# Two parts of a norm in one tile, and four operand tiles that begin 8, 16 or 24 bytes later

## The chip, the core and the metric

One core of a Trainium2 chip runs the kernel. The metric is the device time of one execution in microseconds; for the kernel before it is the median of three runs. A second source is one profiled execution, whose trace gives every instruction's start and duration, engine by engine. Engines are named as the profile names them: PE is TensorE's matmul row, PEld the row of its weight loads, DVE is VectorE, ACT ScalarE, POOL GpSimd, SP the engine whose queue issues most loads.

## The reference

256 tokens of width 1024 pass through two blocks. What matters here is where a norm's output is used as a matmul operand:

```
n1   = rmsnorm(h, norm1_g);  proj = n1 @ w_in          # first block, 40 weight tiles
n2   = rmsnorm(h, norm2_g);  peer: n2 @ w_q, then n2 . expert_u for 128 x 128 experts
x    = x + 0.5 * g1x * swiglu(modulate(rmsnorm(x)), w13_ffn1, w2_ffn1)     # same for ctx
u    = modulate(rmsnorm(x)) @ w_in_2                   # "XN"; the same for ctx, "XC"
x    = x + 0.5 * g3x * swiglu(modulate(rmsnorm(x)), w13_ffn2, w2_ffn2)
out  = rmsnorm(x, norm_final)
```

## The kernel before

Everything lies feature-major: 128 features on the partitions, 8 feature chunks, 256 tokens along the free dimension. Each fp32 operand is split into a high and a low fp32r part (hi + lo), and a product takes three matmuls: hi by whi, lo by whi, hi by wlo (lines 249 to 251). The weights stream through three `raw` buffers of 128 x 1024; ACT copies each to `whi` (line 112), DVE takes the remainder as `wlo` (line 113). A weight tile then serves 24 matmuls of 256 token columns, one weight load of 128 columns each. The order of the work is a list written out by hand; `Emit.run` walks through it, so nothing is scheduled anew.

Five kinds of tiles supply the moving columns or the stationary weights that this case is about. A norm's output is the pair `nhi`, `nlo` made by `npair`: n1 in the first block, n2 for the queries and the 128 expert tiles, then a pair for the context's first norm, then XN for the second block's mixing stage, all in the same place one after the other. `y` is the unnormed product x times gain with two more columns for the modulation's shift, 258 in all: both feed-forward stages start on it before their norm is known (`ypair`, `unit_y`); the context's mixing norm XC lies in the same tile with 256 columns. `nxh`, `nxl` hold the feed-forward's normed input, `ah`, `al` (and `mh`, `mch`, `fohi`, `mhi` and the like) the inputs of the products behind. In the `tm` products (lines 425 to 427) the norm is the stationary operand and 512 columns of weights move.

Tiles are allocated at multiples of 32 bytes of a partition, and the table `GAP` puts unused tiles of 64 to 192 bytes ahead of some. Worked out from the program: `whi` and `wlo` begin 96 bytes past a multiple of 256, n, y, ah, al, mch, fo and m 32 bytes past a multiple of 256, all of them so 32 bytes past a multiple of 64, and a chunk of a norm (1024 bytes) or of y (1280 bytes) keeps that.

Of the kernel before, what the change touches and what calls it, by code (L numbers as in the profile page):

```python
# [12 lines left out]
F32R = mybir.dt.float32r  # L13
# [7 lines left out]
P = 128  # L21
T = 256
D = 1024
KD = D // P
# [12 lines left out]
TS = 320  # L37

GAP = {"n": 48, "ya": 40, "y": 48, "mc": 0, "nx": 32, "q": 48, "v": 16, "sc": 48, "y01": 0, "fo": 40, "f2": 32, "mh": 48}

NE = 7

# [160 lines left out]
def body(ctx, tc, I, out):  # L203
# [6 lines left out]
    npool = ctx.enter_context(tc.tile_pool(name="npool", bufs=1))  # L210
# [17 lines left out]
    def table(func):  # L228

        act.activation(out=dummy, in_=one, func=func)  # L230
# [5 lines left out]
    def V(name):  # L236
        w = dict(VEC)[name]
        return vec[:, VOFF[name]:VOFF[name] + w]
# [16 lines left out]
    def scr(wk, shape=(P, 512)):  # L255
        return wk.tile(list(shape), F32, name="scr", tag="scr", bufs=NSCR[wk.name])


    def ones_sum(qs, bank=bankB):
        ps = bank()  # L260
        for j, q in enumerate(qs):
            for a in range(2):
                pe.matmul(ps[:, :T], ones, q[:, a * T:a * T + T], start=j + a == 0, stop=a == 1 and j == len(qs) - 1)  # L263
        return ps
# [60 lines left out]
    def late_norm(x, r, gain, n, of, when, shift=None, lag=1):  # L325

        def f(d):
            hi, lo = n()
            t = of(d)
            dve.scalar_tensor_tensor(out=t, in0=x[:, d, :], scalar=gain[:, d:d + 1], in1=r, op0=ALU.mult, op1=ALU.mult)  # L330
            if shift is None:
                em.later(lambda: act.copy(hi[:, d, :], t))
                em.later(lambda: dve.tensor_tensor(out=lo[:, d, :], in0=t, in1=hi[:, d, :], op=ALU.subtract), lag)
                return
            sh = shift[:, d:d + 1]
            em.later(lambda: act.activation(out=hi[:, d, :], in_=t, func=AF.Identity, bias=sh))
            em.later(lambda: dve.scalar_tensor_tensor(out=lo[:, d, :], in0=t, scalar=sh, in1=hi[:, d, :],
                                                      op0=ALU.add, op1=ALU.subtract), lag)
        for d in range(KD):
            if when is None:  # L340
                f(d)
            else:
                em.later(lambda d=d: f(d), when[d])
# [7 lines left out]
    def root(ps, scale=1.0 / D, bias=None):  # L351
        r = npool.tile([P, T], F32, name="rr", tag="rr", bufs=1)
        act.activation(out=r, in_=ps[:, :T], func=AF.Sqrt, bias=(eps if bias is None else bias)[:, 0:1], scale=scale)
        return r
# [14 lines left out]
    def gap(pl, name):  # L369
        if GAP[name]:  # L370
            pl.tile([P, GAP[name]], F32, name="gap" + name, tag="gap" + name)

    def chunked(t, w, first=0):

        step = T if w == T else TS
        return t[:, first:first + KD * step].rearrange("p (k t) -> p k t", k=KD)[:, :, 0:w]

    def npair(pl, tag):
        return [chunked(pl.tile([P, KD * T], F32R, name=tag + n, tag=tag + n), T) for n in ("hi", "lo")]

    def apair():
        return [npool.tile([P, T], F32R, name=n, tag=n, bufs=2) for n in ("ah", "al")]
# [206 lines left out]
    hT = {}  # L589
# [62 lines left out]
            nc.sync.dma_start(out=kT[n], in_=I[("k1", "k2")[n]])  # L652

    gap(npool, "n")
    n1 = npair(npool, "n")

    def begin(fetch):
        his, lows, squares, S["q"] = parts(x0, V("norm1_g"), Y1(), pa)
# [334 lines left out]
    def norm2():  # L993
        S["r"] = root(ones_sum(S["q"][:1]))
        table(AF.Gelu_apprx_tanh)
        dve.reciprocal(out=S["r"], in_=S["r"])
        hT["n2"] = npair(npool, "n")
        late_norm(hres, S["r"], V("norm2_g"), X2, lambda d: hres[:, d, :], [0, 0, 0, 0, 0, 1, 1, 1])

    units += [("w", I["wo"][k], wout(k)) for k in range(KD)]  # L1000
# [292 lines left out]
    def first_units(sp):  # L1293
        ps = [q_bank(n) for n in range(2)]
        mm3s([p[:, :T] for p in ps], sp, *Y1(), T)
        em.later(norm2, 1)
# [10 lines left out]
    for j in range(NQ, 16):  # L1307
        n = min(j - 1, sc + (3 if j > NQ else 0))
# [50 lines left out]
    def flat(t):  # L1359
        return t.rearrange("p a t -> p (a t)")  # L1360
# [46 lines left out]
    E_ = {}  # L1407
    Ex = ExitStack()

    def open_pd():  # L1410
        Gx.close()
        Sx.close()
        pd = Ex.enter_context(tc.tile_pool(name="pd", bufs=1))
        E_["p"] = pd
        E_["x"] = pd.tile([P, KD, T], F32, name="x")
        h1 = pd.tile([P, KD, T], F32, name="h1")
        E_["h1"] = h1
        pool.dma_start(out=h1, in_=hD)


        fg = V("final_g")
        w = pd.tile([P, KD], F32, name="w", tag="gain", bufs=3)
        dve.tensor_tensor(out=w, in0=fg, in1=fg, op=ALU.mult)
        dve.tensor_scalar(out=w, in0=w, scalar1=EPS, scalar2=None, op0=ALU.add)
        E_["w"] = E_["x"][:, 0:4, :].rearrange("p a (b i) -> p (a b) i", i=P)
        dve.tensor_copy(E_["w"], w.unsqueeze(2).to_broadcast([P, KD, P]))
        g = gain_of(pd, "norm_ffn1_2", 8)
        dve.tensor_tensor(out=g, in0=g, in1=fg, op=ALU.mult)
        E_["g"] = g
        open_d()  # L1430
        E_["y"] = ypair()
        shift_parts(0, E_["y"])

    def ypair(width=T + 2):
        y = M["p"].tile([P, 2 * KD * TS], F32R, name="y", tag="y", bufs=1)
        return chunked(y, width), chunked(y, width, KD * TS)

    def done_c():
        pd, x, h1, fg = E_["p"], E_["x"], E_["h1"], V("final_g")
# [55 lines left out]
    def nc_pair():  # L1495
        B["n"] = npair(npool, "n")

    second = [ev(b) for b in range(64, P - 2)]
    n = len(ADA_A)
# [22 lines left out]
    def add_to_x(acc, hg):  # L1522
        x = E_["x"]

        def add(d):
            dve.scalar_tensor_tensor(out=x[:, d, :], in0=acc.o(d), scalar=hg[:, d:d + 1], in1=x[:, d, :],
                                     op0=ALU.mult, op1=ALU.add)
        return add
# [28 lines left out]
    M = {}  # L1557
# [32 lines left out]
    def x_sums(func):  # L1590

        em.later(lambda: qsum(E_["q"]))

        def f():
            E_["r"] = root(ones_sum(E_["q"][:1], bankA))
            table(func)
            dve.reciprocal(out=E_["r"], in_=E_["r"])
        em.later(f, 3)

    def f1_done(acc):  # L1600
        x = E_["x"]
        add = add_to_x(acc, E_["hg"])
        for d in ORDER:
            add(d)

        def squares():
            table(AF.Sqrt)
            E_["q"] = [scr(E_["p"]) for _ in range(4)]
            for j, q in enumerate(E_["q"]):
                act.activation(out=q, in_=flat(x[:, 2 * j:2 * j + 2, :]), func=AF.Square)  # L1610
            x_sums(AF.Exp)

        def norm():
            E_["n"] = npair(npool, "n")
            late_norm(x, E_["r"], E_["g"], XN, lambda d: scr(E_["p"])[:, :T], range(KD), modx[:, 24:32])
        em.later(squares, 1)
        em.later(norm, 9)
# [16 lines left out]
    def ctx_done():  # L1634
        hg = E_["p"].tile([P, KD], F32, name="hgc")
        dve.tensor_scalar(out=hg, in0=modc[:, 16:24], scalar1=0.5, scalar2=None, op0=ALU.mult)
        for d in ORDER:
            dve.scalar_tensor_tensor(out=M["ctx"][:, d, :], in0=accc.o(d), scalar=hg[:, d:d + 1],
                                     in1=M["ctx"][:, d, :], op0=ALU.mult, op1=ALU.add)
        M["nc"] = ypair(T)  # L1640
        a, q, b, c = ctx_norm("norm_mix_2", 24, lambda: M["ctx"], lambda: [scr(E_["p"]) for _ in range(4)], XC)
        em.later(lambda: (table(AF.Sqrt), a()))
        em.later(q, 1)
        em.later(lambda: (b(AF.Exp), c(range(KD))), 4)
# [304 lines left out]
    def mixout(k):  # L1949
        def fn(hi, lo):  # L1950
            if k == KD - 3:
                x_prep("norm_ffn2_2", 48, 40, 1.0, lambda: ypair())
            accm.step(hi, lo, M["m"][0][:, k, :], M["m"][1][:, k, :], k == 0, k == KD - 1)
            if k == KD - 1:
                x_parts(accm)
        return fn
# [153 lines left out]
def _program(arrays):  # L2110
    nc = _bacc.Bacc("TRN2", target_bir_lowering=False, num_devices=1)
    aps = {n: nc.dram_tensor(n + "_dram", v.shape, F32, kind="ExternalInput").ap() for n, v in arrays.items()}
    out = nc.dram_tensor("out_dram", (P, KD, T), F32, kind="ExternalOutput").ap()
    with _tile.TileContext(nc) as tc:
        body(tc, aps, out)
    return nc
# [8 lines left out]
```

## Time and profile before

| | |
|---|---|
| median of 3 runs | 1956.73 us (1954.03 to 1963.48) |
| the profiled execution's own time | 1958.64 us |
| its span | 1956.9 us |
| PE busy | 1943.4 us of the span, 15,348 matmuls |
| DVE, ACT, POOL busy | 1392.2, 1016.6, 153.2 us |
[...]

Matmuls overlap: one of 256 columns is shown with 276 to 288 ns, but the next begins some 0.11 us after it starts. What counts is the pace, from start to start. In a window, the count of instructions holds those that begin in it and the two or so that are still running when it opens.

### The profile page before, as it was taken

The page shows a single profiled execution, that of the slowest core. Times are in us where ns is not written, and L with a number is a line of the kernel's source. Part 1 is how long each engine was busy: PE and PEld are TensorE (multiplying, and loading weights), DVE is VectorE, ACT ScalarE, POOL GpSimd, SP SyncE. Part 2 cuts the span into 40 slices and gives each one's busy share as a digit, 9 for nine tenths or more (in the row PEclk, how much of TensorE's full clock was granted, in tenths as well). Part 3 has the DMA queues.
Part 4 walks back from the last instruction along what each step waited for, and adds up shares of the span by engine and source line. Part 5 has one row for each costly group of instructions (what it writes and reads, how often), then busy time and mean ns, then how long its engine had stood idle before and what let it go on. Part 6 is the DMA issues. An engine that isn't in the chain of part 4 may idle for free.

```text
span 1956.9 us, 37794 instructions
## 1 busy us (share of the span) xinstructions
PE 1943.4 (99%) x15348; PEld 1865.1 (95%) x15348; DVE 1392.2 (71%) x2282; ACT 1016.6 (52%) x1510; POOL 153.2 (8%) x296
## 2 busy tenths in 40 slices
PE   9999999999999999999999999999999999999998
PEld 8899999999999999999998888899999999999998
DVE  7667788987776776798866776489754556578555
ACT  6554645467776555545573323246654445455444
POOL 0000011111112001111000000010000000000000
PEclk9999999999999999999999999999999999999999
DMA  7656577776667778897755666677643334456653
GB/s 244 198 166 187 183 230 230 248 223 197 200 199 248 246 242 275 281 298 248 220 186 192 186 199 211 201 249 272 191 130 92 115 110 130 153 174 185 189 188 119
DMA packets 110094, 393.18 MB, mean 201 GB/s; under 512 B 14103, under 2 KB 14487, under 8 KB 109536
## 3 DMA queue, kind: packets, MB, share of 16 engines
q1 hardware_dynamic: 85968, 310.55, 50.6%
q0 software_dynamic: 22944, 77.52, 12.1%
q8 instruction: 120, 1.97, 0.4%
q10 hardware_dynamic: 1008, 2.70, 0.4%
q14 instruction: 54, 0.44, 0.1%
HBM read 371.84 MB, written 18.87 MB: 200 GB/s over the span
## 4 chain that ended last, share of the span: by engine, by line
PE 95%; DVE 2%; ACT 1%; DMA 1%; issue 0%; SPq 0%; DVEq 0%; ACTq 0%
PE wk L249 18%; PE wk L251 18%; PE wk L250 18%; PE acc L250 10%; PE acc L251 10%; PE acc L249 10%; PE acc L425 2%; PE acc L427 2%; PE acc L426 2%; PE acc L1255 1%; PE acc L1256 1%; DVE wlo L113 1%; ACT whi L112 1%; DMA raw<-w_dram 0%; PE wk L263 0%
## 5 line engine op out<-in xcount | busy, mean ns | idle before, releaser
L113 DVE TENSOR_TENSOR wlo<-raw,whi 128x1024 fp32r<-128x1024 f32 x587 | 716.6, 1224 | 463.5 <-ACT whi L112 462.3
L112 ACT CAST whi<-raw 128x1024 fp32r<-128x1024 f32 x587 | 615.6, 1050 | 652.5 <-PE wk L250 285.6
L249 PE MATMUL wk<-nhi,whi 128*128 128x256 f32 x1648 | 464.2, 282 | 0.0
L250 PE MATMUL wk<-nlo,whi 128*128 128x256 f32 x1648 | 456.4, 277 | 0.0
L251 PE MATMUL wk<-nhi,wlo 128*128 128x256 f32 x1648 | 456.2, 277 | 0.0
L250 PE MATMUL acc<-al,whi 128*128 128x256 f32 x1376 | 383.2, 279 | 0.2 <-DVE al L386 0.2
L249 PE MATMUL acc<-ah,whi 128*128 128x256 f32 x1376 | 383.1, 278 | 0.0
L251 PE MATMUL acc<-ah,wlo 128*128 128x256 f32 x1376 | 382.9, 278 | 0.0
L249 PEld LDWEIGHTS wk<-nhi,whi 128*128 128x128 f32 x1648 | 309.7, 188 | 0.9 <-issue 0.5
L250 PEld LDWEIGHTS wk<-nlo,whi 128*128 128x128 f32 x1648 | 310.0, 188 | 0.5 <-issue 0.5
L251 PEld LDWEIGHTS wk<-nhi,wlo 128*128 128x128 f32 x1648 | 309.8, 188 | 0.0
L250 PEld LDWEIGHTS acc<-al,whi 128*128 128x128 f32 x1376 | 260.2, 189 | 1.7 <-DVE al L386 0.8
L249 PEld LDWEIGHTS acc<-ah,whi 128*128 128x128 f32 x1376 | 258.3, 188 | 0.9
L251 PEld LDWEIGHTS acc<-ah,wlo 128*128 128x128 f32 x1376 | 259.0, 188 | 0.0
L249 PE MATMUL wk<-nxh,whi 128*128 128x512 f32 (+1 forms) x544 | 189.2, 348 | 0.0
L251 PE MATMUL wk<-nxh,wlo 128*128 128x512 f32 (+1 forms) x544 | 188.4, 346 | 0.0
L250 PE MATMUL wk<-nxl,whi 128*128 128x512 f32 (+1 forms) x544 | 187.4, 344 | 0.0
L385 ACT CAST ah<-early 128x256 fp32r<-128x256 f32 x128 | 52.1, 407 | 157.1 <-PE acc L251 155.3
L251 PEld LDWEIGHTS wk<-nxh,wlo 128*128 128x128 f32 x544 | 102.1, 188 | 14.1
L250 PEld LDWEIGHTS wk<-nxl,whi 128*128 128x128 f32 x544 | 103.1, 190 | 12.6
L249 PEld LDWEIGHTS wk<-nxh,whi 128*128 128x128 f32 x544 | 102.2, 188 | 11.5
L1269 POOL DMA_DIRECT2D uD<-act x128 | 69.1, 540 | 366.9 <-ACT act L1268 306.6
(526 smaller groups left out, 3343.5 us busy)
## 6 DMA issues: line engine op xcount, KB each, us to landing
raw<-pu_dram SPq DMA_DIRECT2D x128, 512.0 KB, 3.9
raw<-pv_dram SPq DMA_DIRECT2D x128, 512.0 KB, 4.4
row<-ada_dram POOLq DMA_DIRECT2D x59, 512.0 KB, 4.6
raw<-f13a_dram SPq DMA_DIRECT2D x44, 512.0 KB, 3.5
raw<-f2a_dram SPq DMA_DIRECT2D x44, 512.0 KB, 4.6
raw<-f13b_dram SPq DMA_DIRECT2D x44, 512.0 KB, 3.6
raw<-w_dram SPq DMA_DIRECT2D x41, 512.0 KB, 4.1
uD<-act POOLq DMA_DIRECT2D x128, 128.0 KB, 3.9
```

What stands on the lines that cost most here:

```text
L112: nc.scalar.copy(hi, r)
L113: nc.vector.tensor_tensor(out=lo, in0=r, in1=hi, op=ALU.subtract)
L249: pe.matmul(o, whi, xhi, start=start, stop=False)
L250: pe.matmul(o, whi, xlo, start=False, stop=False)
L251: pe.matmul(o, wlo, xhi, start=False, stop=stop)
L385: act.copy(hi, src)
L425: pe.matmul(o, xh[:, k, ts], hi[:, sl], start=k == 0, stop=False)
L426: pe.matmul(o, xh[:, k, ts], lo[:, sl], start=False, stop=False)
L427: pe.matmul(o, xl[:, k, ts], hi[:, sl], start=False, stop=k == KD - 1)
L1255: pe.matmul(o, p2[:, k, :, t], ph[:, k, :, t], start=True, stop=False)
L1256: pe.matmul(o, p2[:, k, :, t], p1[:, k, :, t], start=False, stop=True)
L1269: pool.dma_start(out=uD[:, b, :], in_=u)
```

## The change

`npair` made two tiles, one for each part; it now makes one tile of both parts and 64 elements more, and both parts begin `off` elements further on in it. `ypair` does the same with its tile, which held both parts already. `OFF` gives the elements of 4 bytes: n1 begins 8 bytes later, n2 16, XN 24, y and XC 16. The context's first norm and the pairs `fo` and `m` get the one tile and no offset.

```
+OFF = 2, 4, 6, 4
...
-    def npair(pl, tag):
-        return [chunked(pl.tile([P, KD * T], F32R, name=tag + n, tag=tag + n), T) for n in ("hi", "lo")]
+    def npair(pl, tag, off=0):
+        t = pl.tile([P, 2 * KD * T + 64], F32R, name=tag, tag=tag)
+        return [chunked(t, T, off + n * KD * T) for n in range(2)]
...
-    n1 = npair(npool, "n")
+    n1 = npair(npool, "n", OFF[0])
...
-        hT["n2"] = npair(npool, "n")
+        hT["n2"] = npair(npool, "n", OFF[1])
...
-        y = M["p"].tile([P, 2 * KD * TS], F32R, name="y", tag="y", bufs=1)
-        return chunked(y, width), chunked(y, width, KD * TS)
+        y = M["p"].tile([P, 2 * KD * TS + 64], F32R, name="y", tag="y", bufs=1)
+        return chunked(y, width, OFF[3]), chunked(y, width, OFF[3] + KD * TS)
...
-            E_["n"] = npair(npool, "n")
+            E_["n"] = npair(npool, "n", OFF[2])
```

No instruction is added, removed or moved. Put side by side engine by engine, with the tiles' new names and the line numbers taken as equal, the two programs have the same 22,626 instructions in the same order, and every wait is on the same semaphore for the same value. What differs is where tiles lie. The spare 256 bytes push everything that is allocated later along: ah, al and the first block's tiles by 256 bytes, the tiles above y by 512, the last ones by 1024. Those stay 32 bytes past a multiple of 256 where they were; n1, n2, XN, XC and y do not.

## Rows read from the trace of the kernel before

**Rows 1.** The page's first lines: span, busy time and instructions of each engine.

```profile
span 1956.9 us, 37794 instructions
PE 1943.4 (99%) x15348; PEld 1865.1 (95%) x15348; DVE 1392.2 (71%) x2282; ACT 1016.6 (52%) x1510; POOL 153.2 (8%) x296
```

**Rows 2.** The page's chain that ended last, by engine.

```profile
PE 95%; DVE 2%; ACT 1%; DMA 1%; issue 0%; SPq 0%; DVEq 0%; ACTq 0%
```

**Rows 3.** Windows, PE alone: stretch, its length, busy (count), granted clock, DMA, GB/s.

```profile
260.00:300.00 40.00, 40.00 (x355) 1.00 0.79 248
640.00:700.00 60.00, 60.00 (x532) 1.00 0.77 245
...
850.00:890.00 40.00, 40.00 (x342) 1.00 0.89 290
1766.00:1776.00 10.00, 10.00 (x85) 1.00 0.69 215
1830.00:1930.00 100.00, 100.00 (x852) 1.00 0.60 188
```

**Rows 4.** Groups by line and shape, 77 to 150 us: count, busy us, mean ns.

```profile
L251 PE MATMUL wk<-nhi,wlo 128*128 128x256 f32 x160 | 44.7, 280 | 0.0
```

**Rows 5.** The same view, 219 to 630 us.

```profile
L249 PE MATMUL wk<-nhi,whi 128*128 128x256 f32 x1071 | 302.3, 282 | 0.0
L250 PE MATMUL wk<-nlo,whi 128*128 128x256 f32 x1071 | 296.2, 277 | 0.0
L251 PE MATMUL wk<-nhi,wlo 128*128 128x256 f32 x1071 | 296.0, 276 | 0.0
```

**Rows 6.** The same view, 1353 to 1650 us.

```profile
L251 PE MATMUL wk<-nhi,wlo 128*128 128x256 f32 x336 | 92.9, 277 | 0.0
L250 PE MATMUL wk<-nlo,whi 128*128 128x256 f32 x336 | 92.9, 276 | 0.0
```

**Rows 7.** The same view of the whole run: products on y, and a plain fp32 one.

```profile
L249 PE MATMUL wk<-y,whi 128*128 128x258 f32 x104 | 29.7, 286 | 0.0
...
L318 PE MATMUL wk<-y,whi 128*128 128x258 f32 x32 | 7.9, 287 | 0.5 <-ACT y L289 0.5
...
L251 PE MATMUL acc<-y,wlo 128*128 128x258 f32 x24 | 6.8, 284 | 0.0
...
L263 PE MATMUL wk<-scr,ones 128*128 128x256 f32 x28 | 6.8, 381 | 0.1
```

**Rows 8.** The same view, 1810 to 1945 us.

```profile
L249 PE MATMUL wk<-nxh,whi 128*128 128x256 f32 x224 | 62.9, 281 | 0.0
...
L251 PE MATMUL acc<-ah,wlo 128*128 128x256 f32 x142 | 39.9, 281 | 0.0
```

**Rows 9.** The same view, 629 to 785 us.

```profile
L249 PE MATMUL acc<-ah,whi 128*128 128x256 f32 x455 | 125.6, 276 | 0.0
```

**Rows 10.** The same view, 785 to 900 us.

```profile
L250 PE MATMUL acc<-al,whi 128*128 128x256 f32 x327 | 91.9, 281 | 0.2 <-DVE al L386 0.2
```

**Rows 11.** Instructions of PE in order of time, about 788 us: start us, duration us.

```profile
788.10 0.28 PE L249 MATMUL acc<-ah,whi 128*128 128x256 f32 x1
788.36 0.38 PE L250 MATMUL acc<-al,whi 128*128 128x256 f32 x1
788.58 0.28 PE L251 MATMUL acc<-ah,wlo 128*128 128x256 f32 x1
788.70 0.28 PE L249 MATMUL acc<-ah,whi 128*128 128x256 f32 x1
788.82 0.28 PE L250 MATMUL acc<-al,whi 128*128 128x256 f32 x1
```

**Rows 12.** Instructions on tile cslh: count, duration ns min/median/max, first and last start.

```profile
L249 PE MATMUL wk<-cslh,fth x16: 280/286/290, 1686.4 to 1702.8; 128*128 128x258 f32 x16
```

**Rows 13.** In order of time, about 1764.8 us: three plain fp32 matmuls of a sum.

```profile
1764.78 0.81 PE L263 MATMUL acc<-scr,ones 128*128 128x256 f32 x3
```

**Rows 14.** Instructions on tile nlo: those of DVE that write it.

```profile
L333 DVE TENSOR_TENSOR nlo<-x,nhi x8: 417/418/420, 213.5 to 217.0; 128x256 fp32r<-128x256 f32 x8
```

## The prediction

> **What bounds the kernel now.** I read the page first: PE is busy for 1943.4 of 1956.9 us [rows 1], and the chain that ended last lies on PE for 95% of the span [rows 2]. So the kernel's time is the number of matmuls times their pace, and stalls are small change. Since the change leaves every instruction, order and wait as it was, it can only act by the pace, that is by how fast PE takes its operands from the new places.
>
> The next question is whether the pace is a constant. It is not. A window's count, less the two matmuls that run when it opens, gives it [rows 3]: 40 us by 353 is 113.3 ns from start to start while n2 moves (260 to 300), 60 by 530 is 113.2 ns with ah (640 to 700), but 40 by 340 is 117.6 ns with the very same ah, al and weight buffers at 850 to 890, and 100 by 850 is 117.6 ns in the last feed-forward. [...] There are a fast pace and a slow one, 4.3 ns apart. By groups the same shows as a mean of 276 ns [rows 9] against 281 ns [rows 10], so a group's mean tells which pace a stage had: 276 is fast, 281 is slow, what lies between is a mixture.
>
> What picks the pace is seen at 788 us [rows 11]. Ahead of it starts are 0.11 us apart. Then two matmuls are 0.26 and 0.22 us late, and from there on starts are 0.12 us apart; the mean over the stage behind it is 281 [rows 10]. Same tiles, same bytes: the pace is a state that a pause sets and that then holds. I read it as two streams, the moving columns and the next matmul's weights, that either fall in step or get in each other's way. That is a reading, and no row proves it. With 258 columns the pace is slower again: 10 us by 83 is 120.5 ns on y [rows 3], 7.2 more than the fast pace for two more columns, where 258/256 alone would ask for 0.9.
>
> **The change, part by part.** Nothing is removed or added; each moved stream is priced by what it can gain or lose in pace.
>
> The tile y, 16 bytes on. Its 258-column matmuls are 312 at lines 249 to 251 into wk (three rows like the first), 96 at lines 318 to 323 and 72 into acc, 480 in all [rows 7], means 284 to 287. At the fast pace they would take 113.3 x 258/256 = 114.2 ns instead of 120.5: 6.3 ns by 480, 3.0 us. No row shows 258 columns at the fast pace, so the lower bound of the gain is nothing; the loss, if the new place were as bad again as two more columns, is 7.2 by 480, 3.5 us.
>
> n1, 8 bytes on: 480 matmuls with mean 280 against 276 [rows 4, 9], a gain of 4 ns by 480, 1.9 us if all turn fast; a loss of 2.9 ns each (120.5 less 117.6) would be 1.4 us.
>
> n2, 16 bytes on: 3,213 matmuls between 219 and 630 us, means 277 and 276, so nearly all fast already [rows 5]. (The 282 of line 249 I put down to late starts behind the small fp16 products that stand between, which stay.) The gain left is at most 1 ns each, 3.2 us; I take 1.0. The loss, if they all turned slow, is 4.3 by 3,213, 13.8 us. This is the largest single price in the change.
>
> XN, 24 bytes on: 1,008 moving matmuls with means 277 and 276 [rows 6]: 0.5 us to gain, 4.3 us to lose.
>
> The streams behind. A pace that is set holds until the next pause, and behind y in the last feed-forward come 672 matmuls on nx (three rows of 224) and 528 on ah (22 weight tiles of 24), slow at 281 [rows 8]. If y's stream falls in step, some of these follow: 4.3 by 1,200 is 5.2 us for all of them. The rows give examples of both states after a pause, so I take half, 2.6 us. On the same ground the expert stage may go either way: its 1,365 matmuls ahead of 785 us are fast, the 980 behind it mostly slow [rows 9, 10]. That is 5.9 us to lose and 4.2 to gain, and I take nothing.
>
> The writers. ACT and DVE write the parts to the moved places, 418 ns for a low part [rows 14], and lie beside matmuls; with PE busy 99% they have time to spare [rows 1]. Eight such pieces for each of two parts and four norms: even 5% on each would be 64 x 21 ns, 1.3 us, and under the cover nothing. The tiles that move by 256, 512 or 1024 bytes keep their place within 256; I take nothing for them, by the fact that ah's two buffers (1024 bytes apart) share one mean [rows 9].
>
> The sum: 3.0 + 1.9 + 1.0 + 0.5 + 2.6 = 9.0 us. The profiled execution's 1958.64 us would become 1949.6; it lies 1.9 above the median of the runs, and from that median, 1956.73, the same 9.0 us give 1948.
>
> [...] One piece of the trace reads a 258-column operand from 8 bytes past a multiple of 64: the second half of cslh, whose first half (1032 bytes) begins at such a multiple. Both halves together last 280 to 290 ns with median 286 [rows 12], no other than y's 284 to 287 from its 32 bytes [rows 7]. So 8 bytes cost nothing there that two more columns had not cost already. [...]
>
> **The rivals.**
> *No effect.* Pace depends on where a pause falls, not on bytes, and the states come out as before: 1957, between 1952 and 1962. For it speaks that ah has both paces from one place [rows 9, 10]; against it, that instructions, and so nearly all pauses, are the same in both kernels, so that only places could change anything. [...]
>
> [...]
>
> *Slower.* n2 falls out of step. At 4.3 ns each its 3,213 matmuls cost 13.8 us, with XN's 4.3 it is 18.1: 1975. For it: the whole of n2's stage, with all its pauses for the fp16 products, is fast now from 32 bytes, so that this place looks safe and any other may be less so. From 2,100 slow matmuls on (9.0 by 4.3) it outweighs the forecast's gain. If 16 bytes cost n2 as much as the two columns cost y, it is 7.2 by 3,213, 23 us, and 1980 or more.
>
> **How the numbers follow.** The forecast (slow streams among the moved ones turn fast, fast ones stay): 0.41, 1948, own range 1940 to 1955. Below the fast pace: 0.20, 1925 to 1943. No effect: 0.18. Slower: 0.21, 1965 to 1982. Runs of this kernel spread by some 0.5%, about what tells a change from none, so the classes' bounds are 1947 and 1966.5. About half of the forecast's chance lies under 1947 (0.20) and all of the floor rival's: faster 0.40. The rest of the forecast and no effect make same 0.39, and 0.21 is slower. The range is 1932 to 1974: below it lies a third of the floor rival (0.07), above it the worse half of the slower one (0.11).
>
> **What would show it.** Right: PE's instructions and waits as before, y's means near 278 instead of 284 to 287, n1's near 276, n2's and XN's unchanged, nx's and ah's in the last feed-forward partly 276. [...] The slower one: n2's lines at 281 or more. No effect: all means within 1 ns. The forecast is wrong above all if the pace follows the place in a way the rows cannot show, since every large operand now lies 32 bytes past a multiple of 64.

## The result, and the profile after

The changed kernel took 1980.35 us (median of four runs, 1978.14 to 1981.53), the kernel before 1958.22 beside it (four runs, 1954.03 to 1963.48): a ratio of 1.0114, with an interval of 1.0093 to 1.0135. It is slower by about 22 us. The profiled execution took 1979.81 us, 21.2 more than that of before.

The page of the changed kernel, where it answers to [rows 1, 2]: span, busy time of the engines, and the chain that ended last.

```profile
span 1978.1 us, 37794 instructions
PE 1962.4 (99%) x15348; PEld 1881.7 (95%) x15348; DVE 1392.8 (70%) x2282; ACT 1017.2 (51%) x1510; POOL 153.8 (8%) x296
...
PE 96%; DVE 2%; DMA 1%; ACT 1%; issue 0%; DVEq 0%; ACTq 0%
```

The same instructions and the same chain on PE, with DVE and ACT within 0.6 us of before: what is longer is PE's busy time, by 19.0 of the 21.2 us. So the pace has changed, and the windows tell where. PE alone, as in [rows 3]:

```profile
260.00:300.00 40.00, 40.00 (x338) 1.00 0.76 234
650.00:710.00 60.00, 60.00 (x532) 1.00 0.79 241
1792.00:1802.00 10.00, 10.00 (x84) 1.00 0.66 211
1860.00:1950.00 90.00, 90.00 (x797) 1.00 0.63 194
```

The granted clock is 1.00 in all four, as in [rows 3], and 0.999 in the mean of both profiled executions, so it is not the clock. With n2 moving, 40 us by 336 is 119.0 ns from start to start, where it was 113.3. With ah, whose place stayed, 60 by 530 is 113.2 ns as before. On the 258 columns of y, 10 by 82 is 122 ns (120.5 before). The last feed-forward, 90 by 795, is 113.2 ns where it was 117.6. Groups by line and shape of n2's stage (222 to 646 us), as in [rows 5]:

```profile
L251 PE MATMUL wk<-n,whi 128*128 128x256 f32 x1066 | 306.8, 288 | 0.0
L252 PE MATMUL wk<-n,whi 128*128 128x256 f32 x1066 | 301.2, 283 | 0.0
L253 PE MATMUL wk<-n,wlo 128*128 128x256 f32 x1065 | 300.7, 282 | 0.0
```

All three means are 6 ns higher than before. This is no mixture of the old fast and slow paces: no mean lies under 282, where the slow pace had 281 [rows 8, 10], and the 119.0 ns from start to start lie above the slow pace's 117.6. XN (1369 to 1675 us), 276 and 277 before [rows 6], likewise:

```profile
L252 PE MATMUL wk<-n,whi 128*128 128x256 f32 x334 | 94.6, 283 | 0.0
...
L253 PE MATMUL wk<-n,wlo 128*128 128x256 f32 x333 | 94.1, 283 | 0.0
```

n1 (77 to 148 us), 280 before [rows 4], and its matmuls in order of time (start us, duration us). One group's mean is up by 1 ns only, but the starts tell: from the first row to the last are nine steps in 1.08 us, 120 ns each.

```profile
L252 PE MATMUL wk<-n,whi 128*128 128x256 f32 x160 | 45.6, 285 | 0.0
L253 PE MATMUL wk<-n,wlo 128*128 128x256 f32 x159 | 44.7, 281 | 0.0
```

```profile
139.77 0.28 PE L251 MATMUL wk<-n,whi 128*128 128x256 f32 x1
139.89 0.28 PE L252 MATMUL wk<-n,whi 128*128 128x256 f32 x1
...
140.85 0.28 PE L251 MATMUL wk<-n,whi 128*128 128x256 f32 x1
```

The last feed-forward (1835 to 1965 us), 281 before [rows 8], and y's 258 columns in the whole run [rows 7]:

```profile
L251 PE MATMUL wk<-nxh,whi 128*128 128x256 f32 x224 | 61.8, 276 | 0.0
...
L253 PE MATMUL acc<-ah,wlo 128*128 128x256 f32 x141 | 38.9, 276 | 0.0
```

```profile
L251 PE MATMUL wk<-y,whi 128*128 128x258 f32 x104 | 29.8, 286 | 0.0
```

A finer account comes from the starts in the two traces. For each stage the mean step from one matmul's start to the next was taken (steps over 135 ns, that is pauses, left out; for 512 columns over 270), and the difference multiplied by the stage's count:

| stage | matmuls | ns before | ns after | us |
|---|---|---|---|---|
| n1 (8 bytes) | 480 | 116.6 | 120.1 | +1.7 |
| n2 (16) | 3,216 | 113.9 | 119.2 | +17.1 |
| XN (24) | 1,152 | 113.7 | 120.7 | +8.1 |
| XC (16) | 192 | 113.7 | 119.0 | +1.0 |
| norms as stationary operand, 512 columns | 624 | 229.7 | 232.0 | +1.4 |
| y, 258 columns (16) | 480 | 120.8 | 121.6 | +0.4 |
| ah in the expert stage (not moved) | 3,072 | 114.5 | 113.4 | -3.5 |
| nx and ah of the last feed-forward (not moved) | 1,200 | 117.8 | 113.4 | -5.3 |

The moved streams lose 29.7 us, the two streams at their old places gain 8.8, and the smaller streams together another 1.1. So the paces account for 19.8 of the profiled 21.2 us; the other 1.4 is left to pauses.

### The profile page after: what moved, and what is told of

Same layout as the page of the kernel before. It is cut to its first block, busy times and chain, and to the rows that moved or that the text cites. A ratio compares the mean times of both kernels' runs of the same rounds, so it can differ in the third digit from the quotient of the medians.

```text
span 1978.1 us, 37794 instructions
## 1 busy us (share of the span) xinstructions
PE 1962.4 (99%) x15348; PEld 1881.7 (95%) x15348; DVE 1392.8 (70%) x2282; ACT 1017.2 (51%) x1510; POOL 153.8 (8%) x296
## 4 chain that ended last, share of the span: by engine, by line
PE 96%; DVE 2%; DMA 1%; ACT 1%; issue 0%; DVEq 0%; ACTq 0%
PE wk L251 19%; PE wk L253 18%; PE wk L252 18%; PE acc L252 10%; PE acc L253 10%; PE acc L251 10%; PE acc L428 2%; PE acc L429 2%; PE acc L430 2%; PE acc L1258 1%; PE acc L1259 1%; DMA raw<-pv_dram 1%; DVE wlo L115 1%; ACT whi L114 0%; PE wk L265 0%
## 5 line engine op out<-in xcount | busy, mean ns | idle before, releaser
L251 PE MATMUL wk<-n,whi 128*128 128x256 f32 x1648 | 472.7, 287 | 0.0
L252 PE MATMUL wk<-n,whi 128*128 128x256 f32 x1648 | 466.0, 283 | 0.0
L253 PE MATMUL wk<-n,wlo 128*128 128x256 f32 x1648 | 464.9, 282 | 0.0
L252 PEld LDWEIGHTS wk<-n,whi 128*128 128x128 f32 x1648 | 312.4, 190 | 0.5 <-issue 0.5
L251 PEld LDWEIGHTS wk<-n,whi 128*128 128x128 f32 x1648 | 311.1, 189 | 0.9 <-issue 0.5
L253 PEld LDWEIGHTS wk<-n,wlo 128*128 128x128 f32 x1648 | 311.6, 189 | 0.0
```

The lines of the kernel that those rows point to most:

```text
L251: pe.matmul(o, whi, xhi, start=start, stop=False)
L252: pe.matmul(o, whi, xlo, start=False, stop=False)
L253: pe.matmul(o, wlo, xhi, start=False, stop=stop)
```

## The experiments

Two theories stood first. *Boundary*: an operand must begin at a multiple of 32 bytes. *Relation*: PE's pace depends on how far the moving operand lies from the stationary weights that are loaded meanwhile (PEld is busy for 95% of the span beside PE's 99% [rows 1]); before, that distance was 192 bytes modulo 256 for all streams of 256 and 258 columns (32 less 96, worked out from the program). Where 512 columns move, it was 64. The rival to both was that the shared tile or the 256 bytes of push cost the time. Worked out from the programs, all kernels below have the instructions of before in the same order with the same waits, and differ in addresses alone; so a time that differs is not due to how their tiles are cut. In all of them the line numbers are a few off those of before, and where no other is given the kernel is the changed one with the edit shown. A pace is read from a window as above, length by count less two; where a whole stage's pace is given, it is the mean step as in the table above.

**e1, no offsets.** What is left of the change is the shared tile and the push.

```
-OFF = 2, 4, 6, 4
+OFF = 0, 0, 0, 0
```

> One tile for both parts, as in the change, but all four offsets 0; everything behind still pushed by 256 bytes or more. Boundary theory (a moving operand that does not begin at a multiple of 32 bytes is read slower, whatever the weights' place): 1957 us, n2's three lines at 276 to 282 ns as before. Relation theory (the pace follows the distance between moving operand and weights): the same, since the distance is that of before. Rival, the push: the shared tile or the 256 bytes cost the time, then about 1980 here too. Rival, chance: the states of pace fall anew, 1950 to 1965.

Measured: 1955.79 us (1952.99 to 1964.89), ratio to before 0.9993 (0.9977 to 1.0010). n2's groups (222 to 646 us) and a window of it:

```profile
L253 PE MATMUL wk<-n,wlo 128*128 128x256 f32 x1071 | 296.3, 277 | 0.0
```

```profile
260.00:300.00 40.00, 40.00 (x355) 1.00 0.78 249
```

n2 is back at 113.3 ns. The shared tile and the push cost nothing; the offsets are the whole loss. In this execution nx and ah of the last feed-forward went at 113.3 and 113.5 ns too, with both operands at the places (modulo 256) where before had 117.8: their gain in the changed kernel is no effect of the offset. Seven of the kernels here (the changed one, e1, e2, e4, e7, e8 and e9) have nx and ah at the very same addresses, and this stage took 113.4 ns in five of them and 117.8 and 117.6 in e2 and e7; so one place has both paces. That the pace also changes from one execution of one kernel to the next is not shown, since each kernel has one trace, but the spread of their times goes with it. Against e1's profiled execution, 1952.99 us, in which those streams were fast too, the changed kernel's is 26.8 us longer: the moved streams cost more than the 21.2, and the states gave some of it back.

**e2, every offset 32 bytes**, so that all moved operands begin at a multiple of 32, even of 64.

```
-OFF = 2, 4, 6, 4
+OFF = 8, 8, 8, 8
```

> All four offsets 8 elements, 32 bytes: the moved tiles begin at a multiple of 64 instead of 32 past it. Boundary theory with 32 bytes: 1957 us, 1950 to 1963, n2 at the fast pace of 113 ns. [...] Relation theory: the distance to the weights is off by 32, more than in the change, so 1975 or more and n2 over 281 ns.

Measured: 1979.10 us (1978.29 to 1981.27), ratio 1.0098 (1.0081 to 1.0115). The window in n2:

```profile
260.00:300.00 40.00, 40.00 (x340) 1.00 0.75 239
```

40 by 338 is 118.3 ns. A round address doesn't help, so the boundary theory fell.

**e3, the weights 32 bytes on and the moving operands where they were.** A pad of 32 bytes ahead of the weight buffers, and the pad ahead of the norms shortened by as much.

```
-GAP = {"n": 48, ...
+GAP = {"w": 8, "n": 40, ...
-OFF = 2, 4, 6, 4
+OFF = 0, 0, 0, 0
...
+    splp.tile([P, GAP["w"]], F32, name="gapw", tag="gapw", bufs=1)
```

> Offsets 0; the weight tiles whi and wlo lie 32 bytes further on (128 past a multiple of 256 instead of 96) and the unused tile ahead of n is 32 bytes smaller, so that nothing else moves. Boundary theory: 1957 us, 1950 to 1963, all groups as before. Relation theory: all streams change their distance to the weights, so the means of n, ah, nx and y all move, by 20 us or more in the time.

Measured: 1999.06 us (1997.13 to 2001.12), ratio 1.0198 (1.0180 to 1.0215). Windows in n2 and in ah's stage:

```profile
260.00:300.00 40.00, 40.00 (x343) 1.00 0.76 238
660.00:720.00 60.00, 60.00 (x508) 1.00 0.73 232
```

117.3 ns with n2 and, pauses included, 118.6 with ah. No moving operand was touched, and every stream of 256 columns that had gone at the fast pace became slower, ah as well, which no offset of the change reaches; the last feed-forward, slow before, stayed about where it was, 117.5 ns against 117.8. It is the weights' place relative to the moving operand, or else the weights' own place; e5 tells these apart.

**e4, the doses mixed:** n1 4 bytes, n2 8, XN 16, y 24.

```
-OFF = 2, 4, 6, 4
+OFF = 1, 2, 4, 6
```

> Offsets 1, 2, 4, 6 elements: n1 4 bytes, n2 8, XN 16, y and XC 24. In the change the paces read 120.0 ns at 8 bytes (n1), 119.2 at 16 (n2), 120.7 at 24 (XN). Boundary theory: the pace goes with the offset, not with the stage: n2 now 120.0, XN 119.2, n1 about 120; time 1980 to 1988. Stage or chance theory: n2 keeps 119.2 and XN 120.7 whatever the offset.

Measured: 1988.02 us, one run (before had a median of 1959.88 beside it). The window in n2:

```profile
260.00:300.00 40.00, 40.00 (x335) 1.00 0.74 234
```

n2 at 8 bytes goes at 120.1 ns, what n1 had from there; XN at 16 bytes at 119.1 (mean of its steps), what n2 had from there; n1 at 4 bytes at 121.6. The price belongs to the offset and not to the stage.

**e5, weights and moving operands 32 bytes on together.**

```
-OFF = 2, 4, 6, 4
+OFF = 0, 0, 0, 0
...
+    splp.tile([P, 8], F32, name="gapw", tag="gapw", bufs=1)
```

> Offsets 0; the weights and every moving tile lie 32 bytes further on together, so that all begin at a multiple of 64 and every distance is that of before. Relation theory (the pace follows the distance of moving operand and weights modulo 64): 1957 us, 1950 to 1965, n2 at 113.3 ns a matmul. Rival, absolute places (each operand wants to begin 32 bytes past a multiple of 64): about 2000 us as with the weights moved alone, n2 at 118.

Measured: 1959.85 us (1954.15 to 1964.43), ratio 1.0015 (1.0000 to 1.0031). The window in n2:

```profile
260.00:300.00 40.00, 40.00 (x355) 1.00 0.79 249
```

113.3 ns. The weights lie where e3 had them and the moving operands where e2 had n2, and each of those alone cost 1 to 2%. Together they cost nothing that can be told: of the place what counts, for steps of 32 bytes, is the distance.

**e6, weights and norms 16 bytes on, by larger weight tiles.**

```
-OFF = 2, 4, 6, 4
+OFF = 4, 4, 4, 4
-                hi = self.split.tile([P, 1024], F32R, name="whi", tag="whi")
+                hi = self.split.tile([P, 1040], F32R, name="whi", tag="whi")[:, 4:1028]
```

(`wlo` likewise, and the pad ahead of the norms shortened to 16 elements.)

> All four offsets 16 bytes, and the weights begin 16 bytes further on too (each weight buffer is 64 bytes larger, the unused tile ahead of n smaller, the rest stays modulo 256). Relation theory: n1, n2, XN and XC are back at 113.3 (or the slow state's 117.8) ns, while ah, nx, mch, fo, m, which stay, go to about 119 ns; time near 1990. Absolute theory: n2 stays at 119, and the weights off a multiple of 32 slow the rest too, 2000 or more.

Measured: 2001.20 us, one run (before had a median of 1955.97 beside it). The window in n2:

```profile
260.00:300.00 40.00, 40.00 (x341) 1.00 0.75 232
```

118.0 ns, and ah 282 in the mean: a miss. I had taken the distance modulo 64. The six buffers, now 64 bytes longer each, began 48, 112, 176 or 240 bytes past a multiple of 256, so that the norms had the old distance modulo 64 but mostly not modulo 256. That form of the theory fell; e7 and e10 try the other. The trace shows a limit of the other form: in a third of n2's weight tiles two matmuls out of three lay at the distance 192, and from the first of them to the second it took 117.5 ns in the mean (353 steps). So two matmuls at a good distance, between others that are not, don't bring the fast pace back.

**e7, multiples of 64 bytes:** n1 64, n2 128, XN 192, y 64.

```
-OFF = 2, 4, 6, 4
+OFF = 16, 32, 48, 16
```

> Offsets 64, 128, 192 and 64 bytes (n1, n2, XN, y and XC): all distances keep their value modulo 64 and change modulo 256. Relation modulo 64: 1957 us, 1950 to 1965, n2 113.3 to 113.9 ns, XN 113.7. Relation modulo 256: n1 and y (now at the weights' own place modulo 256) or n2 and XN leave 113.3, by 4 ns or more, 2 to 14 us.

Measured: 1978.29 us (1977.50 to 1980.07), ratio 1.0113 (1.0093 to 1.0134). The window in n2:

```profile
260.00:300.00 40.00, 40.00 (x342) 1.00 0.77 237
```

117.6 ns at 128 bytes; n1 at 64 had 119.9, XN at 192 had 119.0. A period of 64 bytes or of 128 would have made at least one of them fast throughout, as XN and n2 are in e1; one of 256 is not excluded, since e1's push moved tiles by 256, 512 and 1024 at no cost.

**e8, n2's offset alone.**

```
-OFF = 2, 4, 6, 4
+OFF = 0, 4, 0, 0
```

> Only n2 keeps its 16 bytes; n1, XN, y at 0. Relation theory: n2 at 119.2 ns against 113.9, 3216 matmuls, so 16.8 us slower than before, 1970 to 1977, and XN, n1 as before. Chance: n2 near 114 or other stages changed.

Measured: 1976.83 us (1969.70 to 1977.00), ratio 1.0108 (1.0087 to 1.0128). The window in n2:

```profile
260.00:300.00 40.00, 40.00 (x338) 1.00 0.75 237
```

XN's group (1369 to 1675 us), 277 before as well:

```profile
L253 PE MATMUL wk<-n,wlo 128*128 128x256 f32 x336 | 92.9, 277 | 0.0
```

n2 goes at 119.0 ns as with the whole change, while n1 (116.6) and XN (113.7) had their paces of before. n2 alone carries 17.1 us. The profiled execution, the fastest of the four, is accounted for: 1958.64 + 17.1, less 5.3 for a last feed-forward at 113.4 ns, is 1970.4, and it took 1969.70.

**e9, four more distances:** n1 96 bytes, n2 248, XN 160, y 240.

```
-OFF = 2, 4, 6, 4
+OFF = 24, 62, 40, 60
```

> Offsets 96, 248, 160 and 240 bytes: the distance from the weights to the moving operand, modulo 256, is 32 for n1, 184 for n2, 96 for XN and 176 for y and XC (192 in the kernel before). Distance theory modulo 256 with 192 as the one good place: all four slower than before, n2 119 to 122 ns a matmul, XN and n1 117 to 120, y's 256-column products 119 or so, time 1975 to 1990. Rival: 192 is only one good place of several, then one of these stages shows 113.3 ns.

Measured: 1980.18 us, one run beside 1961.34 of before. The window in n2:

```profile
260.00:300.00 40.00, 40.00 (x335) 1.00 0.74 232
```

120.1 ns at n2's distance of 184, 8 short of the good one (it also begins 8 past a multiple of 16, of which e12 tells more); XN at 96 bytes of distance had 120.0, XC at 176 had 119.3, n1 at 32 had 117.2. There was no second good place among them.

**e10, the weights follow the norms by 16 bytes**, with all six weight buffers cut from one tile, so that they stay 1024 bytes apart. n1, n2, XN and y are 16 bytes on too; ah, nx, fo and m stay behind.

```
-OFF = 2, 4, 6, 4
+OFF = 4, 4, 4, 4
...
+        t = self.split.tile([P, 6 * 1024 + 8], F32R, name="w", tag="w", bufs=1)
+        self.w = [t[:, 4 + 1024 * i:4 + 1024 * (i + 1)] for i in range(6)]
...
-                hi = self.split.tile([P, 1024], F32R, name="whi", tag="whi")
+                hi = self.w[ns % 3 + 0]
```

(`wlo` likewise, and the pad ahead of the norms shortened by 32 bytes.)

> All four offsets 16 bytes, and all six weight buffers 16 bytes further on as well (cut from one tile, so that all stay alike modulo 256); ah, nx, mch, fo, m stay. Distance theory modulo 256: n1, n2, XN and XC are back at distance 192 and at the paces of before, n2 113.9 ns; ah, nx, mch, fo and m come to distance 176 and leave 113.3 (113.4 for ah in the expert stage) for 118 to 121. Rival, the moved tiles' own places are what is slow: n2 stays at 119.2 and ah at 113.4 to 114.5.

Measured: 1978.40 us, one run beside 1961.34. Windows in n2 and in ah's stage, and n2's group (230 to 600 us):

```profile
260.00:300.00 40.00, 40.00 (x355) 1.00 0.80 247
660.00:720.00 60.00, 60.00 (x508) 1.00 0.76 232
```

```profile
L255 PE MATMUL wk<-n,w 128*128 128x256 f32 x976 | 268.6, 275 | 0.0
```

The loss has changed sides: n2 goes at 113.3 ns from the very place that cost it 17 us, and ah, which nobody moved, at 118.6. With before and the changed kernel this makes all four pairs of weights at 96 or 112 past a multiple of 256 and moving operand at 32 or 48: fast at 96 with 32 and 112 with 48, slow at the other two. It is the cleanest evidence for the distance, in one run and its trace. It shows another thing: n1 had 113.9 here, under the 116.6 it had before.

**e11, everything 16 bytes on**, weights, norms, y, ah, nx, mc, mh and the small tiles, each cut from a tile with `SH` elements ahead; every distance is again that of before. Its core, beyond e10:

```
+    SH = 4
...
+        if "t" not in AP:
+            AP["t"] = npool.tile([P, 4 * T + 64], F32R, name="a", tag="a")
+        n = AP["n"] = 1 - AP.get("n", 1)
+        return [AP["t"][:, SH + T * k:SH + T * k + T] for k in (n, 2 + n)]
```

> Everything moves together: the weights and every moving tile (n, y, ah, al, nx, mc, fo, m, mh, the branches' y, y01, y23) begin 16 bytes further on, so that each distance to the weights is that of the kernel before. Distance theory alone: 1957 us, 1950 to 1965, fast and slow states mixed as before, 0.998 to 1.002. If at this place the fast state also holds better, as the 114 to 113.4 ns of n1, XN and the 227 ns of the 512-column products in the run with weights and norms moved by 16 hint: 1935 to 1950, with ah and nx at 113.3 in most stages. Absolute places: over 1975.

Measured: 1940.30 us (six runs, 1939.10 to 1942.45), ratio to before 0.9916 (0.9901 to 0.9931): faster than both kernels. Windows, and nx's group of the last feed-forward (1800 to 1940 us):

```profile
260.00:300.00 40.00, 40.00 (x356) 1.00 0.81 256
660.00:720.00 60.00, 60.00 (x532) 1.00 0.78 242
```

```profile
L255 PE MATMUL wk<-nx,w 128*128 128x256 f32 x224 | 61.6, 275 | 0.0
```

n2 and ah were fast before and are so here. The gain is that nearly nothing is slow any more: n1 116.6 to 114.0 ns, nx with 512 columns 229.2 to 227.0, ah of the first feed-forward 117.7 to 114.6, all from the mean steps, and the last feed-forward 113.4 against the 117.8 that before had in its profile.

**e12, the same with 8 bytes**, to tell distance from place.

```
-SH = 4
+SH = 2
```

> The same with 8 bytes instead of 16. Distance theory alone: 1957 us, 1950 to 1965. [...]

Measured: 2032.87 us (2032.24 to 2034.22), ratio 1.0390 (1.0369 to 1.0410), the slowest of all. Windows in n2 and ah:

```profile
260.00:300.00 40.00, 40.00 (x334) 1.00 0.72 230
660.00:720.00 60.00, 60.00 (x502) 1.00 0.75 235
```

120.5 and 120.0 ns at the good distance of 192. So the place does count, below 16 bytes: with weights and moving operand both 8 past a multiple of 16, a matmul costs 6.7 ns and more, at a distance that is otherwise good.

**e13, everything 48 bytes on**: e11 with 32 bytes of pad ahead of the weights. The question was whether e11's gain came from one particular place or from lying 16 past a multiple of 32.

```
 SH = 4
...
+    splp.tile([P, 8], F32, name="gapw", tag="gapw", bufs=1)
```

> As the run with everything 16 bytes further on, and 32 bytes more: weights and moving tiles begin 16 bytes past a multiple of 64 instead of 48, distances as before. If what counts beside the distance is to begin 16 bytes past a multiple of 32: 1940 us again, 1937 to 1944, the slow pace gone. If it is 48 bytes past a multiple of 64: both paces return, 1952 to 1964.

Measured: 1942.20 us (1941.51 to 1942.98), ratio 0.9928 (0.9911 to 0.9944), the same gain. The window in n2:

```profile
260.00:300.00 40.00, 40.00 (x355) 1.00 0.78 256
```

Both places 16 past a multiple of 32 are fast nearly throughout (of the stages with 300 or more matmuls of 256 columns, ah of the first feed-forward is the slowest in both, 114.6 and 114.5 ns); both places at such a multiple (e1's and e5's) give 1953 to 1965 us from one execution to the next.

The distances measured, worked out from the programs: moving operand less weights, modulo 256, for 256 columns, with the mean step of the stage that had it.

| distance, bytes | ns |
|---|---|
| 192 | 113.3, or 117.8 at PE's other pace; stages of both lie between |
| 196, 200 | 121.6, 120.1 to 120.4 |
| 208, 216, 224 | 119.0 to 119.2, 120.7, 118.3 |
| 0, 32, 64 | 119.7 to 119.9, 117.2, 117.8 |
| 96, 128, 160 | 120.0, 119.0, 117.3 to 120.0 |
| 176, 184 | 118.6 to 119.3, 120.0 |

At 184, 196, 200 and 216 the moving operand begins 4 or 8 past a multiple of 16, so these may hold two costs, which no run tells apart; in the others weights and moving operand begin at a multiple of 16. At 32, 64 and 224, and in most stages at 160, the step is within 0.6 ns of the other pace at 192; whether these distances set a pace of their own or only keep the fast one away is not told apart. And the table is for 256 columns: with 512, nx took 229.2 ns at 64 in before and 227.0 in e11, against 233.3 at 32 (e3) and 232.5 at 48 (e10), and the norms' products 227.4 at 0 (e7), so what is good for 256 columns is no rule for 512.

## Why the prediction was wrong, point by point

**PE bounds, and the change acts by the pace alone.** Right: same instructions, same chain, and 19.0 of 21.2 us are PE's busy time.

**The pace is a state that a pause sets, and a moved stream can only change from slow to fast.** This is the step that failed. The forecast was "slow streams among the moved ones turn fast, fast ones stay". So n2, the largest moved stream and fast already, stood in the sum with a gain of 1.0 us, and its loss stood only in a rival. That there are two paces at one place is true, and e1 shows it again. But whether a stream can have the fast pace at all depends on its distance to the weights: at the 13 other distances measured, stages of 256 columns took 117.2 to 121.6 ns. Before, all large streams of 256 columns lay at the one good distance, so no row of it could show the dependence; the last sentence of the prediction's working names this gap, and it decided.

**n2, 1.0 us gained.** Measured +17.1 of loss. The prediction had the price as its "slower" rival at 4.3 ns each, 13.8 us; it was 5.3 ns. That rival came nearest with its 1975 us. Its condition (32 bytes safe, any other place less so) was half right: e5 and e2 show that it is not the 32 bytes but the distance. Its last sentence even has "1980 or more", by y's price of 7.2 ns on n2 alone; that this is the measured time is luck, since n2 paid 5.3, XN 7.0, and streams that were not moved gave 9.9 us back.

**n1 and XN, 1.9 and 0.5 us gained.** Measured +1.7 and +8.1 of loss. Both begin 8 past a multiple of 16 and have a wrong distance besides: 120.1 and 120.7 ns. The prediction's largest price for XN was 4.3 us.

**y, 3.0 us gained.** Measured +0.4 of loss, inside its bounds. In all 15 kernels its 258 columns took 119.5 to 121.6 ns, while XC, 256 columns in the same tile, had 113.7 before: the slow pace there belongs to the two more columns, and no place tried took it away.

**The streams behind y, 2.6 us of 5.2 gained.** They gained 5.3, but not for the reason given: y never fell in step, and e1 and e8 had the same gain with y at its old place. That the sum had a gain here was luck.

**The expert stage, nothing taken.** It gained 3.5 in the profiled execution, within the 4.2 allowed for; with e1 also 113.4 and with e8 114.4, it is the state again.

**Writers, and pushes by multiples of 256: nothing.** Right: the pushes by e1 at 0.9993, the writers by the changed kernel's own page, DVE and ACT 0.6 us longer each.

**The cslh piece as evidence that 8 bytes cost nothing.** It misled. With 258 columns the pace is already 120 ns [rows 3], and on such a stream a bad place hardly shows: y lost 0.8 ns from a place that cost n2 5.3. Besides, both halves of cslh lie away from 192, at 32 and 40 bytes from fth (worked out from the program), so no good place was compared with a bad one. At 192, in e12, a place 8 past a multiple of 16 did cost, for both operands together, 6.7 ns and more on 113.3.

**The rivals.** "No effect" fell with the 22 us, and e3 and e5 show places at work: moving the weights by 32 bytes cost 2.0% alone, and nothing that can be told when the moving operands went with them. "Below the fast pace" fell too. No run shows a pace of 256 fp32r columns that its 1925 to 1943 us, and with them half of the 0.40 for faster, could rest on: in the 15 kernels profiled no stage's mean step for 256 columns went under 113.3 ns.

What stays open: what makes the distance count. The runs show paces, not whether a read of either operand is held up, nor why just 192 is free for 256 columns; nor whether a matmul's own weights count or those loaded for the next, which lay at one distance in every kernel but e6. Distances that are no multiple of 4, or between those in the table, were not tried. Nor is it shown why 16 past a multiple of 32 keeps the pace of 117.8 ns away. And 8 bytes were tried on moving operands alone and on both together, never on the weights alone.

## What to carry to other kernels

When PE is busy all the time, compare the pace from start to start with the best pace for the same shape in the same trace, and compute where in a partition both operands begin. If a stream is slow at full clock, move weights and moving operand separately and then together, in steps of 16 bytes; here, for 256 fp32r columns, the distance of 192 modulo 256, with both 16 past a multiple of 32, took 0.8% off a kernel whose instructions didn't change. Before changing the size of any tile, look at what it does to the addresses behind it: 16 bytes on one operand cost 1.1%.

## What the hardware showed unexpectedly

With the granted clock at 1.00 in every window shown, and 0.998 or 0.999 in the mean of every profiled execution, a stage of 256 columns took from 113.3 to 121.6 ns a matmul with the same instructions and other addresses, and the whole kernel from 1940.30 us (e11) to 2032.87 (e12), 4.8% apart, with 8 bytes as the only difference. With all streams of 256 columns at the distance 192, the spread goes with the place too: at multiples of 32 bytes the ten runs of e5 lay between 1954.15 and 1964.43, at 16 past them all ten of e11 and e13 between 1939.10 and 1942.98.
